# A hybrid decoder layer on one NeuronCore: another order of seven products, later background work at block seams, and other join and queue choices

## The chip, the cores and the metric

The kernel runs on one core of a Trainium2 chip. The metric is device time in microseconds: the median of three runs, 2982.76 us before the change (2982.41 to 2986.3).

## The reference

One layer of a decoder trunk is computed for a prompt of 2048 + 16 tokens and for 8 sample sequences of 8 tokens, with D = 1024 channels and F = 2816 hidden channels, all in float32:

```python
h = rmsnorm(x, norm1_g)
z = h @ w_in                                   # D -> 5D: za, zg, zp, gate_a, gate_b
a = za * sigmoid(zg)
a = layernorm(causal_dwconv(a, width 31) + conv_b)
a = silu(a) @ w_conv_out
p = trailing means of zp over 2/4/8/16 positions, minus zp; per-group linear map, scale
m = sigmoid(gate_a) * a + sigmoid(gate_b) * p
x = x + m @ w_out
h2 = rmsnorm(x, norm2_g)
up = causal_dwconv(h2 @ w_up, width 3)         # D -> 2F: value and gate
x = x + (gelu(gate) * value) @ w_down
y = rmsnorm(x, final_g)
```

The last rows of the convolution inputs, of the pooling inputs and of the up-projected rows are returned too.

## The kernel before

**Tiling.** Channels lie on the 128 partitions, in `KC` = 8 chunks; tokens lie along the free dimension. The tokens are cut into three blocks `b` = 0, 1, 2 of about 704 to 708 columns; the last holds the samples. A matmul has 128x128 weights and about 352 columns, half a block, so that one output chunk of a projection (a *unit*) is 8 chunks x 2 halves x 3 matmuls = 48 matmuls. Three, because each float32 product is made from a rounded high part and a low rest: low weight x high data, high x low, high x high (`gemm`). High and low parts are made by ACT (copy to fp32r) and DVE (subtract); weights are split once and written to DRAM (`keep`), and later blocks load both parts, 1 MB for a unit.

**Order of the units.** For each block: the projections for the convolution gate and value (`G_first`, `G`), the pooling inputs and gates (`PG`, with units `zp`, `wp`, gates), the convolution's output (`C`), the output projection (`WO`), the feed-forward part (`FF`, with up-projections `up` or `pair`, and down-projections `DN`). A block ends with its last `DN`, and the next block's `PG` follows: this is a block *seam*. For block 0 and block 2, `WO` and parts of the rest run in two halves of the columns, `FIRST` and `SECOND`. `join(first)` puts the units made since `first` into one group: their matmuls are then issued in turns, one chunk of each, instead of one unit after the other.

**Pairs.** In block 2, from the fourth hidden chunk on, value and gate of one hidden chunk are made together (`pair`): the 2x2 blocks of weights and data give four products' worth of work with seven products P1 to P7 of 12 matmuls each (Strassen's scheme in Winograd's form). `mixed_weights` prepares the sums of weight blocks in the background (tiles `raw`, stores `keep<-s`), and stores them as `m1` to `m4`. The seven products accumulate in four PSUM regions: `x` and `a` are the two halves of tile `ps1`, `bb` and `d` those of `ps2`. `sums` reads them back: `u` is made from `d`, `ug` (gate) from `u` and `bb`, `uv` (value) from `x`, `u` and `a`. `g_conv` and `v_post` apply the width-3 convolution, `g_conv` GELU too, and `fg_post` multiplies and splits.

**What sets the order.** The program is laid out by a planner while it is built. `Pace` keeps an estimated time for each engine; the costs are in the helpers (`tt`, `stt`, `act`, `load`, `store`, `mm`). Matmuls are issued unit after unit, and between units (inside a group, between turns) `drip` issues steps of background tasks as long as the estimated DVE time is behind TensorE's. A task may have a unit from which on it may start (`mark[...]`). `force` issues the rest of a task that a unit needs. Each engine works through its own queue in order; so do the DMA queues of SP (`load`) and POOL (`store`).

**Weights.** `w_loads` requests the weights of coming units: those that lie in DRAM in split form up to two units past the oldest unit in work (`LEAD` = 4), into four buffers (`W_BUFS`, tile `wb`). Two `raw` buffers take unsplit weights, and are shared with `mixed_weights`.

**Background tasks that the change touches.** `final(b)` makes y of block b (tiles `s`, stores `out_y`); `x_again(b)` loads the residual x of a block for `WO`, in which `add_post` adds it; `mixed_weights` is described above. The rsqrt of each norm is made with small matmuls, `ones` (column sums) and `cst` (spreading the result), with DVE steps on tile `rs` between them.

Of the kernel before, what the change touches and what calls it, by code (L numbers as in the profile page):

```python
# [133 lines left out]
def trunk(ctx: ExitStack, tc: tile.TileContext, A, O):  # L134
# [72 lines left out]

    def store(dst, src):
        nc.gpsimd.dma_start(out=dst, in_=src)  # L209
        move = size(src) * P * 4 / 340.0  # L210
        pace.put("pool", 1000.0, [], [src], late=2000.0 + move)
        pace.free["dma"] += move
# [563 lines left out]

    def x_again(b):
        for c in range(KC):
            R["x1", b, c] = x_load(b, c)
        yield  # L780

# [105 lines left out]
    def mixed_weights():  # L887
# [5 lines left out]
        for f in range(PLAIN, FC):  # L893
            yield from room(MIX_ROOM)
            v, g = (pace.alloc("raw", RAW_BUFS, wpool.tile([P, 2 * h], F32, tag="raw", name=nm("raw"), bufs=RAW_BUFS)) for _ in range(2))
            load(v, A["w_up"][f])
            load(g, A["w_up"][FC + f])
            a11, a12, a21, a22 = v[:, :h], v[:, h:], g[:, :h], g[:, h:]
# [16 lines left out]
            yield from part(a12, "m3", 0, 2 * h)  # L915
            yield from part(a22, "m3", h, 2 * h)
            s3 = S(h)
# [8 lines left out]
            yield from part(a11, "m2", h, 2 * h)  # L926
            yield from part(a12, "m4", 0, h)

# [55 lines left out]
    def pair(b, f):  # L984
# [9 lines left out]
        def mmf(_):  # L994
# [39 lines left out]
            def sums():  # L1034
                u = pu[:, n:]
                yield from ready(4)
                yield at(d)
                for k in ("c1", "c5", "c7"):
                    done(box[k])
                tt(u, pq[:, :n], d, ALU.add)  # L1040
                ug = S(2 * n)
                tt(ug[:, n:], pq[:, n:], pu[:, :n], ALU.add)
                tt(ug[:, n:], ug[:, n:], u, ALU.add)
                yield from ready(5)
                yield at(x)
                uv = S(2 * n)
                act(uv[:, :n], x, AF.Copy)
                yield from ready(6)
                yield at(bb)
                tt(ug[:, :n], u, bb, ALU.add)  # L1050
                two = lambda t: t.rearrange("p (a c) -> p a c", a=2)
                yield from g_conv(b, f, BOTH, two(ug))
                del ug
                yield from ready(7)
                yield at(a)
                tt(uv[:, n:], u, a, ALU.add)
                box.clear()
                del u
                yield at(uv)
                yield from v_post(b, f, BOTH, two(uv))  # L1060
                del uv
                yield from fg_post(b, f, BOTH)
# [21 lines left out]
            prod(x, 2, 0, b21, False)  # L1084
            box["n"] = 5
            yield
            for t in older:
                done(t)
            if pres[1]:
                pres[1]()  # L1090
            prod(bb, 2, h, mx[4], False)
            w_start(w[3])
            box["n"] = 6
            yield
            prod(a, 3, 0, b22, False)
            w_start(w[3] + 1)
# [8 lines left out]
    def final(b, ts_):  # L1105
        c0, c1 = cols(b, ts_)
        r = yield from (rstd_ps if b == NBLK - 1 and ts_[-1] == 1 else rstd_of)(x_part(b, ts_, "x2n"), c1 - c0)
        for c in range(KC):
            x = R["x1", b, c][:, c0:c1]
            o = wide(x, r) if len(r.shape) == 3 else x  # L1110
            calm = lambda: b == NBLK - 1 or pace.free["dma"] < pace.free["pe"]
            yield "room", calm
            stt(o, o, col(O_FG + c), r, ALU.mult, ALU.mult)
            store(O["y"][c, :, COL0[b] + c0 : COL0[b] + c1], x)
            if ts_[-1] == 1:
                del R["x1", b, c]
            yield
# [69 lines left out]
    def G_first(own):  # L1187

        halves = [(("h1", 0, FIRST),), (("h1", 0, SECOND),)]
        ws = [w_gate(0), w_value(0), w_gate(1)]  # L1190
        for ts_, nd in zip(SPLIT, halves):
            i = len(units)
            gate(0, 0, ws[0], nd, ts_)
            value(0, 0, ws[1], nd, ts_)
            join(i)
            gate(0, 1, ws[2], nd, ts_)
        n0, n1 = halves[1], (("h1", 1),)
        value(0, 1, w_value(1), n0)
        for c in range(2, KC):
# [30 lines left out]
    def PG(b, nd, ga):  # L1230
# [21 lines left out]
        zs = [c for g in POOL_ORDER for c in (2 * g, 2 * g + 1)]  # L1252
        for k in range(3):
            zp(zs[k])
        if b:
            join(i)
        zp(zs[3])
        for k, g in enumerate(POOL_ORDER):
# [27 lines left out]
    def WO(b, parts):  # L1286
        mark["WO", b] = len(units)
        for ts_ in parts:
            for c in range(KC):
                std_unit(  # L1290
                    W(("out", c), A["w_out"][c]), lambda: R["m", b], b, ts_,
                    lambda ps, c=c, ts_=ts_: add_post(b, c, ts_, ps, "x1n"), (("x", b),), wait=c == 0,
                    drop=("m", b) if ts_ == parts[-1] and c == KC - 1 else None,
                )

    def up(b, m, w, nd, ts_=BOTH, hold=None):
# [85 lines left out]
    for b in range(NBLK):  # L1382
# [5 lines left out]
        add_task(("s", b), silu(b), mark["mid", b] if b else mark["C", 0] - 2, [("cv", b)])  # L1388
        add_task(("x", b), x_again(b), mark["WO", b])
        for ts_ in parts.get(b, (BOTH,)):  # L1390
# [3 lines left out]
        for ts_ in SPLIT if b == NBLK - 1 else (BOTH,):  # L1394
            add_task(("y", b, ts_), final(b, ts_))
        if b + 1 < NBLK:
# [7 lines left out]
    add_task(("hist",), histories(), mark["WO", NBLK - 1])  # L1404
    add_task(("mw",), mixed_weights(), mark["PG", 1])

# [214 lines left out]
```

## Time and profile before

| | |
|---|---|
| median of three runs | 2982.76 us |
| the profiled execution | 2985.01 us |
| its span | 2983.2 us |
| TensorE (PE) busy | 2918.1 us, 98% |
| VectorE (DVE) busy | 2034.3 us, 68% |
| ScalarE (ACT) busy | 817.5 us, 27% |
| GpSimd (POOL) busy | 380.2 us, 13% |
| mean granted TensorE clock | 0.990 |
| DMA | 660.13 MB, mean 221 GB/s |

The profile lists each engine's instructions with start, duration, code line and the tiles written and read (`out<-in`, buffer numbers left out), and for an idle stretch what ended it. Most operations are recorded under the line of their helper: L215 is `mm`, L181 `tt`, L185 `stt`, L196 `act`, L205 `load`, L209 `store`. A busy TensorE is not one at full clock: the clock that was granted is given as a share, in stretches. A wait for several things is put down to the one that came last by the profile; where the engine named had long been done, it was another, often a DMA.

### The profile page before, as it was taken

To read this page: it belongs to the slowest core of one execution; us is meant where nothing else is said; L and a number is where in the kernel's file an instruction comes from. 1 tells how busy PE (TensorE), PEld (TensorE's weight loads), DVE (VectorE), ACT (ScalarE), POOL (GpSimd) and SP (SyncE) were. 2 spreads that over 40 slices of the span, in tenths; PEclk is the share of its full clock that TensorE was granted. 3 is DMA by queue.
4 is the path that set the end of the run, shared out by engine and by line. 5 is a ranking of instruction groups with operands and counts; after the bars stand their busy time and mean duration, and the time that the engine had idled before them with its cause. 6 is when DMAs were issued, how large, how long until landed. Compare 5 with 4: busy or idle time off the path is not lost.

```text
span 2983.2 us, 44492 instructions
## 1 busy us (share of the span) xinstructions
PE 2918.1 (98%) x17928; PEld 2906.2 (97%) x17928; DVE 2034.3 (68%) x3006; ACT 817.5 (27%) x1238; POOL 380.2 (13%) x730
## 2 busy tenths in 40 slices
PE   7999999999999999999999999999999999999997
PEld 7999999999999998999999999999999999999997
DVE  7998998679997456643499999646652136544645
ACT  4201334233223233522211213213241013221312
POOL 1111110020010102232110000222210010000001
PEclk9999999999999999999999999999999999999998
DMA  7424554965655657798643344879754384778786
GB/s 282 150 84 160 198 209 165 333 220 174 232 189 208 212 200 296 276 331 294 231 162 146 123 152 144 300 268 313 283 187 143 141 302 168 261 268 263 259 289 232
DMA packets 155501, 660.13 MB, mean 221 GB/s; under 512 B 24992, under 2 KB 29216, under 8 KB 113440
## 3 DMA queue, kind: packets, MB, share of 16 engines
q1 hardware_dynamic: 107280, 433.21, 43.0%
q0 software_dynamic: 48016, 224.09, 19.0%
q8 instruction: 141, 2.31, 0.3%
q14 instruction: 64, 0.52, 0.1%
HBM read 433.17 MB, written 224.05 MB: 220 GB/s over the span
## 4 chain that ended last, share of the span: by engine, by line
PE 85%; DVE 6%; issue 3%; DMA 3%; ACT 2%; POOL 1%; SPq 0%; DVEq 0%; POOLq 0%; ACTq 0%
PE ps L215 85%; DVE s L185 4%; DVE s L181 1%; DMA wb<-keep 1%; ACT s L196 1%; DVE wb L181 1%; POOL keep L209 1%; DMA raw<-in_w_in 1%; DMA raw<-in_w_up 0%; DMA s<-in_x 0%; DMA keep<-s 0%; ACT wb L196 0%; DMA raw<-in_w_out 0%; SPq L205 0%; DVE s L190 0%
## 5 line engine op out<-in xcount | busy, mean ns | idle before, releaser
L215 PE MATMUL ps<-s,wb 128*128 128x354 f32 (+3 forms) x17628 | 2885.0, 325 | 36.5 <-ACT s L196 14.5
L215 PEld LDWEIGHTS ps<-s,wb 128*128 128x128 f32 x17628 | 2867.4, 189 | 46.5 <-DVE s L181 18.2
L185 DVE SCALAR_TENSOR_TENSOR s<-s,half,s 128x704 f32<-128x704 f32 (+1 forms) x720 | 619.6, 925 | 0.0
L196 ACT ACTIVATE s<-s 128x704 fp32r<-128x704 f32 (+10 forms) x447 | 314.6, 711 | 808.2 <-DVE s L185 455.9
L181 DVE TENSOR_TENSOR s<-s,s 128x704 f32<-128x704 f32 (+11 forms) x526 | 400.7, 775 | 98.3 <-ACT s L196 89.9
L181 DVE TENSOR_TENSOR s<-s,ps 128x704 f32<-128x704 f32 (+4 forms) x225 | 158.8, 715 | 288.8 <-PE ps L215 246.8
L196 ACT ACTIVATE s<-ps 128x356 f32<-128x356 f32 (+5 forms) x197 | 117.0, 600 | 683.7 <-PE ps L215 650.7
L185 DVE SCALAR_TENSOR_TENSOR s<-ps,cst,s 128x704 f32<-128x704 f32 (+1 forms) x188 | 178.2, 949 | 110.9 <-ACT s L196 107.2
L209 POOL DMA_DIRECT2D keep<-s x266 | 142.3, 540 | 640.4 <-ACT s L196 507.8
L185 DVE SCALAR_TENSOR_TENSOR s<-s,cst,s 128x708 f32<-128x708 f32 (+4 forms) x188 | 156.0, 842 | 88.0 <-ACT s L196 82.0
L181 DVE TENSOR_TENSOR wb<-raw,wb 128x1024 fp32r<-128x1024 f32 (+3 forms) x136 | 153.0, 1126 | 41.8 <-ACT wb L196 41.2
L196 ACT ACTIVATE wb<-raw 128x1024 fp32r<-128x1024 f32 (+3 forms) x136 | 132.4, 978 | 165.2 <-PE ps L215 88.4
L196 ACT ACTIVATE s<-ps,cst 128x704 f32<-128x704 f32 (+1 forms) x94 | 79.1, 844 | 329.7 <-PE ps L215 322.9
L209 POOL DMA_DIRECT2D keep<-wb x136 | 77.1, 567 | 690.0 <-DVE wb L181 673.6
L185 DVE SCALAR_TENSOR_TENSOR s<-s,ps 128x704 f32<-128x704 f32 (+6 forms) x65 | 43.8, 694 | 147.8 <-PE ps L215 136.1
L185 DVE SCALAR_TENSOR_TENSOR s<-s,s 128x704 f32<-128x704 f32 (+2 forms) x96 | 85.2, 888 | 70.9 <-ACT s L196 68.2
L181 DVE TENSOR_TENSOR s<-raw,s 128x512 fp32r<-128x512 f32 x114 | 74.2, 686 | 33.6 <-ACT s L196 25.7
L196 ACT ACTIVATE s<-raw 128x512 fp32r<-128x512 f32 x114 | 67.6, 623 | 39.4 <-PE ps L215 18.6
L181 DVE TENSOR_TENSOR s<-s 128x718 f32<-128x718 f32 (+6 forms) x64 | 55.1, 861 | 25.8 <-issue 15.3
L209 POOL DMA_DIRECT2D out_ffn_s<-sf x44 | 23.7, 538 | 316.7 <-ACT sf L196 270.3
L185 DVE SCALAR_TENSOR_TENSOR sc<-sa,cst,sc 128x64 f32<-128x64 f32 x232 | 47.0, 279 | 0.3
L196 ACT ACTIVATE s<-s,half 128x704 f32<-128x704 f32 (+1 forms) x48 | 46.3, 971 | 0.8
(61 smaller groups left out, 465.9 us busy)
## 6 DMA issues: line engine op xcount, KB each, us to landing
wb<-keep SPq DMA_DIRECT2D x227, 1024.0 KB, 5.0
keep<-wb POOLq DMA_DIRECT2D x100, 1024.0 KB, 6.4
keep<-s POOLq DMA_DIRECT2D x266, 256.0 KB, 5.2
raw<-in_w_up SPq DMA_DIRECT2D x82, 512.0 KB, 6.4
wb<-keep SPq DMA_DIRECT2D x40, 640.0 KB, 5.1
wb<-keep SPq DMA_DIRECT2D x32, 768.0 KB, 5.4
raw<-in_w_in SPq DMA_DIRECT2D x40, 512.0 KB, 4.6
s<-in_x SPq DMA_DIRECT2D x40, 352.0 KB, 7.7
```

The source lines that it names most:

```text
L181: nc.vector.tensor_tensor(out=out, in0=a, in1=b, op=op)
L185: nc.vector.scalar_tensor_tensor(out=out, in0=a, scalar=s, in1=b, op0=op0, op1=op1)
L196: nc.scalar.activation(out, a, func, **kw)
L209: nc.gpsimd.dma_start(out=dst, in_=src)
L215: nc.tensor.matmul(out, lhsT=lhsT, rhs=rhs, start=start, stop=stop, skip_group_check=again)
```

## The change

Seven edits are made together.

1. In `pair`, P3 into `a` comes sixth and P4 into `bb` seventh (before: P4 sixth, P3 seventh). `m3` and `m4` swap one of their blocks for it, and `sums` does the value side before the gate side.
2. In `PG`, for blocks 1 and 2, two `zp` units are joined instead of three.
3. `final(b)` of blocks 0 and 1 may start only six units after the next block's `PG` begins, and `mixed_weights` six units after that of block 1.
4. `mixed_weights` loads its raw weights through POOL's queue (`load_later`) instead of SP's; in `Pace` a store counts 600 ns of POOL's time instead of 1000.
5. The residual x is loaded by the `WO` units: three chunks ahead of the first unit, then one chunk at each unit, two units early. It was a task that loaded all eight ahead of the first. In `WO` of blocks 0 and 2 the first two units of the first half are joined.
6. In `G_first`, `value(0, 1)` is made in halves, the first of them with the first half's units.
7. The stores of y of the last block go through SP's queue instead of POOL's.

```diff
+    def load_later(out, src):
+        nc.gpsimd.dma_start(out=out, in_=src)
+        move = size(out) * P * 4 / 340.0
+        pace.put("pool", 600.0, [out], [], late=2000.0 + move)
+        pace.free["dma"] += move
-    def store(dst, src):
-        nc.gpsimd.dma_start(out=dst, in_=src)
+    def store(dst, src, last=False):
+        (nc.sync if last else nc.gpsimd).dma_start(out=dst, in_=src)
-        pace.put("pool", 1000.0, [], [src], late=2000.0 + move)
+        pace.put("pool", 600.0, [], [src], late=2000.0 + move)
...
-    def x_again(b):
-        for c in range(KC):
-            R["x1", b, c] = x_load(b, c)
-        yield
+    def x_again(b, c):
+        for k in range(0 if c == 0 else c + 2, min(c + 3, KC)):
+            R["x1", b, k] = x_load(b, k)
...
-            load(v, A["w_up"][f])
-            load(g, A["w_up"][FC + f])
+            load_later(v, A["w_up"][f])
+            load_later(g, A["w_up"][FC + f])
...
-            yield from part(a22, "m3", h, 2 * h)
+            yield from part(a22, "m4", 0, h)
...
-            yield from part(a12, "m4", 0, h)
+            yield from part(a12, "m3", h, 2 * h)
...
-                yield from ready(5)
-                yield at(x)
+                yield from ready(6)
+                yield at(a)
                 uv = S(2 * n)
                 act(uv[:, :n], x, AF.Copy)
-                yield from ready(6)
+                tt(uv[:, n:], u, a, ALU.add)
+                yield at(uv)
+                two = lambda t: t.rearrange("p (a c) -> p a c", a=2)
+                yield from v_post(b, f, BOTH, two(uv))
+                del uv
+                yield from ready(7)
                 yield at(bb)
                 tt(ug[:, :n], u, bb, ALU.add)
...
                 yield from g_conv(b, f, BOTH, two(ug))
                 del ug
-                yield from ready(7)
-                yield at(a)
-                tt(uv[:, n:], u, a, ALU.add)
...
-                yield from v_post(b, f, BOTH, two(uv))
...
-            prod(bb, 2, h, mx[4], False)
+            prod(a, 2, h, b22, False)
             w_start(w[3])
             box["n"] = 6
             yield
-            prod(a, 3, 0, b22, False)
+            prod(bb, 3, 0, mx[4], False)
...
-            store(O["y"][c, :, COL0[b] + c0 : COL0[b] + c1], x)
+            store(O["y"][c, :, COL0[b] + c0 : COL0[b] + c1], x, b == NBLK - 1)
...
-        ws = [w_gate(0), w_value(0), w_gate(1)]
+        ws = [w_gate(0), w_value(0), w_gate(1), w_value(1)]
...
             gate(0, 1, ws[2], nd, ts_)
+            value(0, 1, ws[3], nd, ts_)
...
-        value(0, 1, w_value(1), n0)
...
-        for k in range(3):
+        for k in range(4):
             zp(zs[k])
-        if b:
-            join(i)
-        zp(zs[3])
+            if b and k == 1:
+                join(i)
...
-                    lambda ps, c=c, ts_=ts_: add_post(b, c, ts_, ps, "x1n"), (("x", b),), wait=c == 0,
+                    lambda ps, c=c, ts_=ts_: add_post(b, c, ts_, ps, "x1n"), (), wait=c == 0,
+                    pre=(lambda c=c: x_again(b, c)) if ts_ == parts[0] else None,
...
+                if c == 1 and ts_ == FIRST:
+                    join(mark["WO", b])
...
-        add_task(("x", b), x_again(b), mark["WO", b])
...
-            add_task(("y", b, ts_), final(b, ts_))
+            add_task(("y", b, ts_), final(b, ts_), mark["PG", b + 1] + 6 if b + 1 < NBLK else 0)
...
-    add_task(("mw",), mixed_weights(), mark["PG", 1])
+    add_task(("mw",), mixed_weights(), mark["PG", 1] + 6)
```

More of the change, by code (lines that the diff above doesn't have):

```diff
@@ L1043, in sums @@
                 tt(ug[:, n:], ug[:, n:], u, ALU.add)
-                yield from ready(5)
-                yield at(x)
+                yield from ready(6)
+                yield at(a)
                 uv = S(2 * n)
                 act(uv[:, :n], x, AF.Copy)
-                yield from ready(6)
+                tt(uv[:, n:], u, a, ALU.add)
[4 more added lines that the diff above has]
+                yield from ready(7)
                 yield at(bb)
                 tt(ug[:, :n], u, bb, ALU.add)
-                two = lambda t: t.rearrange("p (a c) -> p a c", a=2)
+                box.clear()
+                del u
                 yield from g_conv(b, f, BOTH, two(ug))
                 del ug
-                yield from ready(7)
-                yield at(a)
-                tt(uv[:, n:], u, a, ALU.add)
-                box.clear()
-                del u
-                yield at(uv)
-                yield from v_post(b, f, BOTH, two(uv))
-                del uv
                 yield from fg_post(b, f, BOTH)
@@ L1084, in mmf @@
             prod(x, 2, 0, b21, False)
-            box["n"] = 5
             yield
```

## The prediction, made before the changed kernel ran

> **What bounds the kernel now.** I read the page first, then TensorE's waits and timeline, then single stretches. TensorE is busy 98% of the span, so only its idle gaps and slow-clock stretches can be won; no matmul is removed.
>
> ```profile
> span 2983.2 us, 44492 instructions
> PE 2918.1 (98%) x17928; PEld 2906.2 (97%) x17928; DVE 2034.3 (68%) x3006; ACT 817.5 (27%) x1238; POOL 380.2 (13%) x730
> ```
>
> All idle time is 2983.2 - 2918.1 = 65.1 us. TensorE's timeline (start, duration, line, operation, count, idle before and what ended it) says where the parts that this edit can reach lie:
>
> ```profile
> 31.57 0.80 PE L215 MATMUL ps<-ones,s 128*128 128x1 f32 x6 [0.87 <-DVE s L181]
> 34.41 1.55 PE L215 MATMUL ps<-cst,rs 128*128 128x128 f32 x6 [2.04 <-DVE rs L185]
> 37.68 0.67 PE L215 MATMUL ps<-s,wb 128*128 128x358 f32 x1 [1.72 <-ACT s L196]
> 553.79 0.66 PE L215 MATMUL ps<-s,wb 128*128 128x352 f32 x1 [2.42 <-ACT s L196]
> 554.72 34.31 PE L215 MATMUL ps<-s,wb 128*128 128x352 f32 x194 [0.26 <-DVE s L181]
> 1173.06 280.79 PE L215 MATMUL ps<-s,wb 128*128 128x352 f32 x1728 [7.24 <-ACT s L196]
> 2153.88 278.52 PE L215 MATMUL ps<-s,wb 128*128 128x354 f32 x1704 [4.92 <-DMA wb<-keep]
> 2465.55 3.90 PE L215 MATMUL ps<-s,wb 128*128 128x356 f32 x12 [2.87 <-DMA wb<-keep]
> 2645.28 13.92 PE L215 MATMUL ps<-s,wb 128*128 128x356 f32 x84 [0.60 <-DVE s L181]
> ```
>
> A gap can cost more than its length. Rows of stretches (bounds, length, busy and count of each engine, granted clock, DMA share, GB/s):
>
> ```profile
> 553.40:560.20 6.80, 6.15 (x20) 5.77 (x21) 2.55 (x3) 2.42 (x4) 0.53 (x1) 0.50 1.02 375
> 560.20:575.00 14.80, 14.80 (x92) 14.80 (x92) 5.94 (x9) 5.09 (x7) 1.60 (x3) 1.00 0.87 324
> 1173.00:1178.00 5.00, 4.94 (x17) 4.97 (x18) 4.08 (x5) 1.90 (x3) 1.83 (x4) 0.50 0.99 338
> 2154.20:2157.60 3.40, 3.40 (x14) 3.40 (x13) 2.44 (x6) 0.90 (x2) 0.78 (x1) 0.50 0.96 370
> 2640.00:2700.00 60.00, 57.60 (x350) 56.41 (x350) 39.22 (x70) 22.43 (x52) 4.84 (x9) 1.00 0.74 263
> ```
>
> At full clock one matmul takes 14.80/92 = 0.161 us. After the three larger gaps the clock is 0.50: 6.15 - 20 x 0.161 = 2.9 us lost at 553, 4.94 - 17 x 0.161 = 2.2 at 1173, 3.40 - 14 x 0.161 = 1.1 at 2154. The 0.60 us gaps of the pairs leave it at 1.00.
>
> The Trainium skill, "TensorE: Matmul & The Clock Gate", Part 1 (the HAM clock gate), has the half clock come after at least one idle window of about 3.4 us. The trace disagrees at 553, where 2.42 us were enough. By the rule the 2.9 us there would not hang on the gap, and the sum below would be 2.9 us smaller, ending at 2954.0. I give it no chance of its own, because the row shows the loss.
>
> **The change part by part.**
>
> *Product order in a pair.* A product is 12 matmuls, 12 x 0.166 = 2.0 us (13.92/84 each). In before the order ends P2, P4, P3; P4 writes `bb`, which shares a PSUM tile with `d`, and DVE still has to read `d` for `u`:
>
> ```profile
> 2643.89 0.90 DVE L181 TENSOR_TENSOR s<-s,s 128x708 f32<-128x708 f32 x1
> 2644.70 0.52 DVE L181 TENSOR_TENSOR s<-s,ps 128x356 f32<-128x356 f32 x1
> 2645.52 0.45 ACT L196 ACTIVATE s<-ps 128x356 f32<-128x356 f32 x1
> 2647.55 0.52 DVE L181 TENSOR_TENSOR s<-s,ps 128x356 f32<-128x356 f32 x1 [0.52 <-PE ps L215]
> 2653.85 0.79 ACT L196 ACTIVATE s<-s 128x708 f32<-128x708 f32 x1
> 2654.53 0.88 ACT L196 ACTIVATE s<-s,cst 128x708 f32<-128x708 f32 x1
> 2655.44 1.95 DVE L185 SCALAR_TENSOR_TENSOR s<-s,cst,s 128x708 f32<-128x708 f32 x2 [3.04 <-ACT s L196]
> 2657.48 0.25 DVE L190 TENSOR_SCALAR s<-sf,cst 128x64 f32<-128x64 f32 x1
> 2657.77 0.60 DVE L185 SCALAR_TENSOR_TENSOR s<-sf,cst,s 128x64 f32<-128x64 f32 x2
> PE ps L215 <- DVE s L181: 9.1, 15, 0.7
> ```
>
> `u` ends at 2644.70 + 0.52 = 2645.22, TensorE goes on at 2645.28, and 2.0 us later DVE adds `bb` (2647.55). The read is late because the previous pair's `fg_post` (2643.89) stands before it in DVE's queue. The last line, TensorE's waits from 2500 to 2921, counts 15 such gaps, 9.1 us. Afterwards P3 stands between: it writes the other tile, whose `x` and `a` were copied long ago, and gives 2.0 us of cover for a gap of 0.60. The older pair's chain moves too: value side from P3's end, gate side from P4's. Counting P4's end as 0: `uv` from -1.9 (0.52), ACT's scaling 0.88, two STT 1.95 and the samples 0.25 + 0.60 bring the value side to 2.3; then `ug` 0.52, ACT 0.88, STT 1.95, samples 0.85, GELU 0.79 and the product 0.90 end at 8.2. The next pair's `d` is ready at 8.0 (four products), so `u` runs from 8.2 to 8.7, and P4, which waits for it, starts only at 12: 3 us of slack. Who waits for the added P3: only the gate side, which DVE could not start before 2.3 anyway. Gain 9.1 us. Ends: 9.1 at best; at worst P3, in the tile that also holds `x`, waits for ACT's copy of `x` (0.45) in each of 19 pairs, which takes 8.6. I take 9.1, as that copy is issued behind P3. After the last pair the longer chain (GELU now last) stands ahead of the last down-projection's fifth row: +0.4, between 0 and 0.8 (GELU's row).
>
> *Seams (`PG` joins two, not three; `final` and `mixed_weights` start 6 units later; raw loads on POOL's queue).*
>
> ```profile
> 1134.61 25.48 SPq L205 DMA_DIRECT2D raw<-in_w_up  x4
> 1163.95 31.25 SPq L205 DMA_DIRECT2D wb<-keep  x7
> wb<-keep SPq DMA_DIRECT2D x1, 1024.0 KB, 9.0
> 2119.33 23.87 SPq L205 DMA_DIRECT2D raw<-in_w_up  x4
> 2143.29 10.45 DMA wb<-keep
> wb<-keep SPq DMA_DIRECT2D x227, 1024.0 KB, 5.0
> ```
>
> ACT is named for the 7.24 us, but that ACT work was long past for a fourth `zp`. Its weights were: issued at 1163.95 (the third row is that load alone), landed 9.0 us later, 1172.95; TensorE started at 1173.06. At the second seam SP stood 23.87 us in four raw loads waiting for buffers; the weight load behind them left at 2143.29 and took 10.45, 2153.74, against 2153.88. A median load takes 5.0. The load window reaches two units past the oldest, so three joined units leave the fourth's load until the group is through. With two joined, the third's weights are there already and cover the fourth's load: 48 x 0.161 = 7.7 us from the group's end, with no raw load ahead on SP and no y burst beside it. 7.7 beats 5.0; at 9.0 some 1.3 us would be left. Gain 7.24 + 2.2 = 9.4 and 4.92 + 1.1 = 6.0. Ends: 0 to 15.4; I take all, since the row of 5.0 is the one without the burst.
>
> What is pushed on: `final`'s 8 STT and 8 stores and the start of the mixed weights move by six units, five of 48 matmuls and one of 24, 264 x 0.161 = 42.5 us, into projections where a DMA share of 0.95 left TensorE busy throughout (first row below). On POOL a raw load stands behind stores that wait for the same DVE subtraction; it adds its issue, 38 times about 0.53 us (4.25/8, the row of the last stores), to a queue that is 13% busy. Behind it wait weight stores and the history copies of `pool_post` (a rival below). The last raw loads are the four at 2119; 42.5 us later is covered by the stretch of the second row, ahead of the pairs:
>
> ```profile
> 1275.00:1350.00 75.00, 75.00 (x468) 75.00 (x467) 32.65 (x47) 21.51 (x34) 23.64 (x45) 1.00 0.95 339
> 2250.00:2325.00 75.00, 75.00 (x465) 75.00 (x464) 10.75 (x12) 8.67 (x11) 0.00 (x0) 1.00 0.39 141
> ```
>
> So nothing; were that cover gone, up to 42.5 us would be forced ahead of the first pair.
>
> *`WO`: first two units joined, x in chunks.* Block 0's first unit has 7 x 3 = 21 matmuls before it needs the last merged chunk, whose `hi` and `lo` end the 2.42 and 0.26 gaps. Joined, another 21 x 0.161 = 3.4 us stand there. 2.68 < 3.4: gain 2.68 + 2.9 = 5.6, ends 2.4 (clock stays slow) and 5.6; I take 5.6. Block 2 shows no gap there. The second unit's post comes one unit later; PSUM has two more slots. Chunks: three x loads ahead, then one per unit two units early, 2 x 24 x 0.161 = 7.7 us, against
>
> ```profile
> 541.08 7.89 SPq L205 DMA_DIRECT2D s<-in_x  x8
> s<-in_x SPq DMA_DIRECT2D x40, 352.0 KB, 7.7
> ```
>
> in a burst of eight. Nothing; without that cover about 1 us. SP's queue gains: a raw output weight no longer waits behind eight x loads (7.89).
>
> *Start.* 24 matmuls (24 x 0.166 = 4.0 us) of `value(0, 1)` now need only the first half and can stand in the gaps of 0.87, 2.04 and 1.72. Put ahead of the `ones` matmuls they fill the first alone; between `ones` and `cst`, the second. Ends 0.9 and 4.0; I take 1.0, the planner's likelier place being ahead.
>
> *Last stores on SP.*
>
> ```profile
> 2974.54 4.25 POOL L209 DMA_DIRECT2D out_y<-s  x8 [10.87 <-DVE s L185]
> out_y<-s POOLq DMA_DIRECT2D x8, 177.0 KB, 2.5
> s<-in_x SPq DMA_DIRECT2D x16, 179.0 KB, 4.1
> ```
>
> POOL's last issue ends at 2978.8 (2974.54 + 4.25), the span at 2983.2, though a store lands in 2.5. On SP the first half's stores wait for DVE; the last down-projection weights are requested ahead of them, so nothing stands behind. No row shows an SP store. From 2.3 us less (it lands as POOL's and the end follows) to 1.6 more (4.1 in place of 2.5); I take 1.0 less. The planner's costs (1000 to 600) only reorder what is issued; I take nothing, and 2 us either way, as the small gaps of the quoted timeline (0.26 to 2.04) are of that size.
>
> **Not touched:** the gap of 2.87 us at 2465 waits for a third up-projection's weights; neither window nor order changes there.
>
> **Sum.** 9.1 - 0.4 + 9.4 + 6.0 + 5.6 + 1.0 + 1.0 = 31.7 us. The profiled execution took 2985.01 us (span 2983.2), so 2953.3 for it; it stands 2.25 above the median of 2982.76, so the median becomes 2982.76 - 31.7 = 2951.1.
>
> **The rivals.**
>
> *Contention stays.* The Trainium skill, "DMA: Bandwidth & Descriptors", Rules for kernel authors, says that spreading DMAs over issuing engines saves issue time only, since all run on the same 16 DMA engines. As a mechanism here: the loads of 9.0 and 10.45 us stay so long because stores still fill the engines (0.99 of their time at 1173 to 1178), and both seam gaps remain or return six units on. Then 31.7 - 15.4 = 16.3, giving 2966.5. For it: the 9.0; against: one unit more of lead, and the stretch at 0.95 without a gap. 14%.
>
> *The pairs' wait only moves.* Tile-wide waits could catch P3 behind the copy of `x`, which is ACT work of 0.45. Then 9.1 is not won: 2960.2. Against: the copy is issued only after P3. 9%.
>
> *POOL's queue blocks (the other side).* Behind a raw load that waits for its buffer stand the small history copies that a `zp`'s post needs. SP's waits of 1100 to 1200:
>
> ```profile
> SPq L205 <- DVE s L181: 18.3, 3, 9.0
> ```
>
> If all of a 9.0 us wait reached TensorE for each of 19 f, 171 us: 2982.8 - 31.7 + 171 = 3122. It decides from 31.7/19 = 1.7 us per f. With one unit (7.8 us) ready meanwhile, 1.2 us x 19 = 23 remains and the kernel is still faster, 2974. Slower 5%.
>
> *No gain:* fresh gaps from the reshuffled plan use up everything, 2983. 4%.
>
> **How the numbers follow.** Forecast 68%; the rivals as above. From no change this kernel is told within about 0.2% (6 us). Contention to 2966.5 and unmoved pairs set the upper end, 2967; below, the full 4.0 at the start and 2.3 at the end (4.3 more), and 2 of the planner give 2945. Faster: 68 + 14 + 9 = 91, less 1 for rivals together: 0.90; same 0.04; slower 0.06.
>
> **What would show it.** Pairs: TensorE's waits from the first pair to the last without the 15 gaps of 0.60. Seams: no gap over 1 us between the first `zp` units and the fifth, clock 1.00 there. `WO`: no gap and no 0.50 at the first output projection. End: SP, not POOL, in the last lines of the chain. Unchanged: the gap before the first joined up-projections of block 2. Wrong, if gaps named "DMA wb<-keep" stand elsewhere, or POOL copies appear in the chain.

## The result, and the profile after

The changed kernel takes 2966.74 us (median; 2964.97 to 2968.08) against 2982.72 for the kernel before in the same series: ratio 0.9943, 95% interval 0.9926 to 0.9961. It is 16.0 us faster; 31.7 were forecast. The profiled execution took 2964.97 us. Its page, the lines for span and engines:

```profile
span 2963.1 us, 44420 instructions
PE 2913.6 (98%) x17928; PEld 2906.4 (98%) x17928; DVE 2034.2 (69%) x3007; ACT 818.3 (28%) x1238; POOL 393.9 (13%) x752
```

TensorE's timeline after the change, where idle time is left or was to go (start, duration, line, operation, count, idle before and what ended it; `issue` means that the profile shows nothing it waited for):

```profile
544.84 37.19 PE L222 MATMUL ps<-s,wb 128*128 128x352 f32 x230
627.50 0.66 PE L222 MATMUL ps<-s,wb 128*128 128x354 f32 x1 [1.81 <-ACT s L196]
892.12 2.68 PE L222 MATMUL ps<-s,ones 128*128 128x352 f32 x4 [4.72 <-DVE s L181]
1636.44 5.83 PE L222 MATMUL ps<-s,wb 128*128 128x354 f32 x25 [3.76 <-issue]
2599.72 60.48 PE L222 MATMUL ps<-s,wb 128*128 128x354 f32 x371
2912.16 0.43 PE L222 MATMUL ps<-s,wb 128*128 128x354 f32 x1 [2.32 <-ACT s L196]
```

The same places as rows of stretches (bounds, length, busy and count of PE, PEld, DVE, ACT, POOL, granted clock, DMA share, GB/s):

```profile
627.50:634.30 6.80, 6.19 (x20) 5.82 (x21) 6.80 (x15) 3.34 (x7) 6.63 (x8) 0.50 0.00 0
890.30:897.10 6.80, 4.97 (x13) 4.01 (x14) 5.04 (x6) 1.85 (x3) 1.07 (x2) 0.50 0.94 321
1150.00:1175.00 25.00, 25.00 (x158) 25.00 (x157) 9.71 (x11) 4.43 (x6) 3.11 (x6) 1.00 0.32 106
1637.80:1641.20 3.40, 3.40 (x14) 3.40 (x13) 1.69 (x3) 2.03 (x3) 0.00 (x0) 0.50 0.00 0
2125.00:2160.00 35.00, 35.00 (x218) 35.00 (x217) 25.32 (x41) 10.80 (x24) 16.66 (x34) 1.00 0.90 313
```

The gap of 553 is gone (544.84 runs 37.19 us unbroken), both seams run full at clock 1.00 (25.00 of 25.00, 35.00 of 35.00, the latter with the DMA engines at 0.90), and 60 us of the pairs have no gap (371 matmuls in 60.48 us). Three stalls are new: at 627, at 892 and at 1636, each with the clock at 0.50 behind it.

To see what each was worth, count all 17928 matmuls in order of time and compare the start of the same number in both traces:

| matmul | before, us | after, us | shift, us | what lies between this row and the one above |
|---|---|---|---|---|
| 200 | 58.49 | 57.10 | -1.4 | start: 1.4 won |
| 3300 | 562.77 | 556.10 | -6.7 | 553: 5.3 won |
| 3700 | 627.66 | 621.51 | -6.2 | |
| 3800 | 646.07 | 643.54 | -2.5 | new stall at 627: 3.6 lost |
| 5400 | 906.14 | 910.96 | +4.8 | new stall at 892: 7.3 lost |
| 7000 | 1163.12 | 1168.83 | +5.7 | |
| 7300 | 1221.10 | 1215.90 | -5.2 | seam 1: 10.9 won |
| 8900 | 1477.63 | 1472.00 | -5.6 | |
| 10000 | 1654.45 | 1654.95 | +0.5 | new stall at 1636: 6.1 lost |
| 13000 | 2137.80 | 2140.51 | +2.7 | |
| 13300 | 2193.07 | 2187.90 | -5.2 | seam 2: 7.9 won |
| 15000 | 2476.24 | 2468.98 | -7.3 | |
| 17600 | 2910.03 | 2891.59 | -18.4 | pairs: 11.2 won |
| end of the span | 2983.2 | 2963.1 | -20.1 | end: 1.7 won |

Won: 1.4 + 5.3 + 10.9 + 7.9 + 11.2 + 1.7 = 38.4. Lost in the three new stalls: 3.6 + 7.3 + 6.1 = 17.0. The unlabelled rows add 1.1 of loss, together 20.3, which rounding takes to 20.1. Every gain of the forecast shows at its place; something took back 17 us. (Such shifts between two single executions carry about 2 us of chance: two kernels below whose TensorE order is the same differ by 2.1 us at matmul 4000. The two spans differ by 20.1 us, the medians by 16.0: the traced execution of before lay 2.3 us above its median, that of the change 1.8 below.)

### The profile page after: what moved, and what is told of

It reads as the page before. It is cut to its first block, busy times and chain, and to the rows that moved or that the text cites. A ratio compares the mean times of both kernels' runs of the same rounds, so it can differ in the third digit from the quotient of the medians.

```text
span 2963.1 us, 44420 instructions
## 1 busy us (share of the span) xinstructions
PE 2913.6 (98%) x17928; PEld 2906.4 (98%) x17928; DVE 2034.2 (69%) x3007; ACT 818.3 (28%) x1238; POOL 393.9 (13%) x752
## 4 chain that ended last, share of the span: by engine, by line
PE 71%; DVE 12%; issue 10%; DMA 3%; POOL 2%; ACT 1%; SPq 0%; DVEq 0%; POOLq 0%; ACTq 0%
PE ps L222 71%; DVE s L185 7%; DVE s L181 3%; DVE wb L181 2%; POOL keep L216 2%; DMA wb<-keep 1%; DMA raw<-in_w_up 1%; DMA keep<-s 1%; ACT s L196 1%; DMA keep<-wb 0%; ACT wb L196 0%; POOL raw L210 0%; DMA s<-in_x 0%; SPq L205 0%; DVE rs L185 0%
## 5 line engine op out<-in xcount | busy, mean ns | idle before, releaser
L181 DVE TENSOR_TENSOR s<-s,s 128x704 fp32r<-128x704 f32 (+11 forms) x526 | 401.1, 775 | 126.2 <-ACT s L196 117.3
L196 ACT ACTIVATE s<-ps 128x356 f32<-128x356 f32 (+6 forms) x197 | 117.3, 601 | 694.3 <-PE ps L222 677.6
```

What stands on the lines that cost most here:

```text
L181: nc.vector.tensor_tensor(out=out, in0=a, in1=b, op=op)
L196: nc.scalar.activation(out, a, func, **kw)
```

## The experiments

Each series ran on one chip together with the kernel before: 2982.22 (first four), 2982.46 (next four), 2981.34 (last four). "Edit" numbers are those of the section on the change; a line of three dots in a code cut stands for lines left out.

**1. Edit 1 alone.** The kernel before with the new order of products:

```diff
 # pair: P3 into a sixth, P4 into bb seventh; sums: value side, then gate side
+            prod(a, 2, h, b22, False)
...
+            prod(bb, 3, 0, mx[4], False)
...
```

> Before, with the new order of the seven products alone. Theory (the pairs' wait sits behind DVE's read of d in P4's tile): all 15 gaps of 0.60 us between the first and the last pair go, TensorE's count through that stretch gets 9 to 10.4 us shorter, nothing else moves, 2982.7 - 9 = 2972 to 2974. Rival (it only moves): gaps of similar size before P2 or P3, 2980 to 2984.

2971.41 us, ratio 0.9970 (0.9958 to 0.9982): 10.8 us, 0.6 below the range of the theory. All 15 gaps of 0.60 are gone. Both seam gaps stay, and at the first one the profile now names the weights, where in the trace before it had named ACT:

```profile
1171.49 8.76 PE L215 MATMUL ps<-s,wb 128*128 128x352 f32 x37 [8.39 <-DMA wb<-keep]
2152.76 7.55 PE L215 MATMUL ps<-s,wb 128*128 128x354 f32 x34 [5.15 <-DMA wb<-keep]
```

The prediction's reading, that the release by ACT was long past and a weight load was the cause, is borne out.

**2. Edit 2 alone.** Two `zp` units joined, not three, in the kernel before:

```diff
-        for k in range(3):
+        for k in range(4):
             zp(zs[k])
-        if b:
-            join(i)
-        zp(zs[3])
+            if b and k == 1:
+                join(i)
```

> Before, with two zp units joined instead of three and nothing else. Theory A (the fourth zp's weights are late at both seams, and what TensorE wins ahead of 1600 us it loses again near 1636, where its PSUM waits for a backlog on DVE): the 7.24 us gap near 1166 shrinks to 1 to 5 us since raw loads still stand on SP, the 4.92 us gap near 2149 stays at 3 to 5 us, and a new gap near 1636 takes most of the first gain: 2979 to 2983. Rival B (gains add up, the gap near 1636 belongs to another edit): no gap near 1636, 2972 to 2978.

2966.40 us, ratio 0.9951 (0.9937 to 0.9966): 15.8 us, from the smallest of the edits, and 5.6 us below the range of B, the nearer theory. SP's queue and TensorE at the first seam, TensorE at the second:

```profile
1155.41 17.02 SPq L205 DMA_DIRECT2D wb<-keep  x4
1164.21 15.97 PE L215 MATMUL ps<-s,wb 128*128 128x352 f32 x98 [0.17 <-DMA wb<-keep]
2134.72 25.45 PE L215 MATMUL ps<-s,wb 128*128 128x354 f32 x156
```

The weight loads begin at 1155, not at 1163.95, and 0.17 us is left of 7.24; the second seam runs through. (In before, 25 us of raw loads stand ahead of the load of 1163.95 in SP's queue. They do not hold it: in experiment 3, without them, it leaves at 1164.20.) `final` and `mixed_weights` still start where they did, so neither had to move for this. There is no stall at 1636 either, as rival B had it: that one belongs to another edit.

**3. Raw loads of edit 4 alone.**

```diff
...
-            load(v, A["w_up"][f])
-            load(g, A["w_up"][FC + f])
+            load_later(v, A["w_up"][f])
+            load_later(g, A["w_up"][FC + f])
```

> Before, with the raw loads of mixed_weights on POOL's queue and nothing else. Theory A: the gap near 2149 goes (6 us with the slow clock), since SP no longer stands in raw loads; the gap near 1166 stays at 5 to 7 us, because there the buffer of the first joined unit and a 9 us landing set it: 2976 to 2978. Rival (the contention of the y burst sets both): both gaps stay, 2982 to 2984.

2990.51 us, ratio 1.0031 (1.0020 to 1.0043): 8 us slower, above both ranges. SP and TensorE at the first seam, then POOL, DVE and TensorE at the second:

```profile
1164.20 20.65 SPq L205 DMA_DIRECT2D wb<-keep  x5
1175.13 5.17 PE L222 MATMUL ps<-s,wb 128*128 128x352 f32 x22 [9.06 <-DMA wb<-keep]
...
2138.97 1.09 POOL L210 DMA_DIRECT2D raw<-in_w_up  x2
2156.15 0.54 POOL L216 DMA_DIRECT2D keep<-s  x1 [0.54 <-DMA out_y<-s]
2156.68 0.21 POOL L201 COPY s<-phist 128x15 f32<-128x15 f32 x1
2156.93 1.73 DVE L181 TENSOR_TENSOR s<-s 128x658 f32<-128x658 f32 x2 [4.99 <-POOL s L201]
2166.45 0.66 PE L222 MATMUL ps<-s,wb 128*128 128x354 f32 x1 [3.13 <-ACT s L196]
```

The first seam keeps its gap, now 9.06 us; at the second the old gap is gone and others come. A history copy of 0.21 us stands behind stores of y and `keep` stores that themselves wait for work on DVE and for other transfers; it runs at 2156.68, DVE waits 4.99 us for it, and TensorE for what DVE and ACT make of it. Before, the same copy ran at 2144.13. This is the prediction's rival "POOL's queue blocks", at one place and not in each of 19 pairs. It is not all of the 8 us: against the trace before, 6.7 us are won at the old gap and 8.3 lost at the new ones there, 1.0 is lost at the first seam and 1.9 at 2097, where TensorE waits 1.76 us for weights. Together that is 4.5; the rest was not found.

**4. The change without edit 5** (x loaded by a task ahead of `WO`, no join in `WO`; the rest as changed):

```diff
...
+        add_task(("x", b), x_again(b), mark["WO", b])
...
-                if c == 1 and ts_ == FIRST:
-                    join(mark["WO", b])
```

> The changed kernel without edit 5 (x loaded as one task, first two output units not joined). Theory A: the 5.3 us won near 553 are lost, the slow clock near 627 (3.6 us) and the 4.72 us gap near 892 (7.9 us with its clock) do not come up, so TensorE reaches 1600 us some 6 us earlier than in the changed kernel, but DVE has as much to do by then, the gap near 1636 grows from 3.76 to about 10 us and the total stays at 2965 to 2968. Rival B (losses add up locally): the gap near 1636 stays at about 3.8 us and the total is 2959 to 2962.

2952.34 us, ratio 0.9902 (0.9887 to 0.9917), against 0.9926 to 0.9961 for the whole change: 14.4 us faster than it, and 6.7 below the lower range, since both theories kept the stall at 1636. TensorE's timeline without edit 5:

```profile
552.22 0.42 PE L222 MATMUL ps<-s,wb 128*128 128x352 f32 x1 [2.55 <-ACT s L196]
553.14 33.04 PE L222 MATMUL ps<-s,wb 128*128 128x352 f32 x194 [0.50 <-DVE s L181]
627.85 1.70 PE L222 MATMUL ps<-s,wb 128*128 128x354 f32 x9
629.85 0.43 PE L222 MATMUL ps<-s,wb 128*128 128x354 f32 x1 [0.30 <-ACT s L196]
631.12 268.60 PE L222 MATMUL ps<-s,wb 128*128 128x354 f32 x1655 [0.83 <-DVE s L181]
```

The gap at 553 is back; the 1.81 us at 627 are 0.30, since nine matmuls (1.70 us) stand there between the norm's `cst` matmuls and the first unit that needs the norm; and 1655 matmuls run from 631 to 900 without the stall at 892. Nor is there one at 1636. So all three new stalls come with edit 5, which in the table wins 5 us and loses 17.

**5. The stall at 892 moved away** in the whole change:

```diff
 # conv_norm, before rsums(acc, W)
-        yield at(acc)
+        yield "at", pace.ready(acc) + (6000.0 if b == 1 else 0.0)
```

> The changed kernel, with one addition: for block 1 the step of conv_norm that issues the column sums (ones) counts as ready 6 us later for the planner, which puts these four matmuls 78 matmuls further back in TensorE's order, where they stood before the change. Theory A (the stall at 892 us is the price of that place in the order, and of nothing else): the gap of 4.72 us and the half clock behind it go, about 7 us, and the stalls at 627 and 1636 stay: 2958 to 2962. Theory B (DVE is late in this stretch whatever the place; the wait returns at the cst matmuls or at the following posts): gaps of 4 to 8 us in all between 890 and 960, 2964 to 2968.

2965.35 us, ratio 0.9940 (0.9924 to 0.9957): no different from the change. Why the place matters: DVE's last two additions in the change, then the same in before, with TensorE's four column sums there:

```profile
890.16 1.81 DVE L181 TENSOR_TENSOR s<-s,s 128x704 f32<-128x704 f32 x2
897.53 1.81 DVE L181 TENSOR_TENSOR s<-s,s 128x704 f32<-128x704 f32 x2
902.34 1.35 PE L215 MATMUL ps<-s,ones 128*128 128x352 f32 x4
```

The additions end at 890.16 + 1.81 = 891.97 and at 899.34. In before the column sums came 3 us later, 902.34. In the change they stand 78 matmuls (78 x 0.161 = 12.6 us) earlier in TensorE's order, and their row, 892.12 with 4.72 idle, is the wait for the additions. With the 78 matmuls given back the gap of 4.72 is gone, and matmul 5500 starts 7.9 us earlier than in the change (1.6 of it from before that place). But the order behind 945 us is the same, and yet new stalls stand at 1969 and 2097, which take it back: at matmul 13000 the kernel is 2.7 us later than the change. For the first of them, ACT, DVE and TensorE:

```profile
1961.35 1.16 ACT L196 ACTIVATE s<-raw 128x512 fp32r<-128x512 f32 x2 [7.56 <-DMA raw<-in_w_up]
1963.89 0.83 ACT L196 ACTIVATE s<-ps,cst 128x704 f32<-128x704 f32 x1
1967.41 1.93 DVE L185 SCALAR_TENSOR_TENSOR s<-ps,cst,s 128x704 f32<-128x704 f32 x2
1969.44 10.82 PE L222 MATMUL ps<-s,wb 128*128 128x352 f32 x56 [3.74 <-issue]
```

ACT waits 7.56 us for a raw weight. A read of PSUM stands behind it in ACT's queue, and DVE, which needs what ACT makes of the weight, has reads of PSUM behind that in its own; these end at 1967.41 + 1.93 = 1969.34, and TensorE goes on at 1969.44. Theory A is right about the cause of the stall at 892. The median lies in B's range, but not for B's reason: between 890 and 960 the largest gap is 0.81 us. How often the new stalls come is not shown: the traced execution took 2969.73 us, 4.4 above the median, and another 2959.59, inside A's range.

**6. Edit 5 alone**, both parts, in the kernel before:

```diff
...
-        add_task(("x", b), x_again(b), mark["WO", b])
...
+                    pre=(lambda c=c: x_again(b, c)) if ts_ == parts[0] else None,
+                if c == 1 and ts_ == FIRST:
+                    join(mark["WO", b])
```

> The kernel before with edit 5 alone: x loaded chunk by chunk and the first two units of WO joined in blocks 0 and 2. Theory A (the edit costs the same alone as in company, 14.4 us net: 5 won at 553, lost at 627, at 892, and at 1636): 2993 to 2999, with the ones matmuls of block 1 waiting near 910 and a new gap between the first seam and the second of block 1's output projection. Theory B (only some of its stalls are its own; the one at 1636 needs the delayed final as well): 2986 to 2991. Theory C (it is a gain alone, its losses come from company): 2976 to 2981.

2987.57 us, ratio 1.0020 (1.0010 to 1.0029): by itself the edit makes the kernel slower by 5 us. The number is B's, but not for B's reason: all three stalls are there, at 629 (1.81), 893 (5.25) and 1646 (3.78), and it loses less than A said because the gap at the second seam, 4.92 us before, is 0.50 here:

```profile
1646.20 203.69 PE L215 MATMUL ps<-s,wb 128*128 128x354 f32 x1248 [3.78 <-issue]
2168.55 267.82 PE L215 MATMUL ps<-s,wb 128*128 128x354 f32 x1649 [0.50 <-DVE s L181]
```

**7. The change without the x chunks** (eight loads ahead of `WO`, as before; the join stays):

```diff
...
+        add_task(("x", b), x_again(b), mark["WO", b])
...
-                    pre=(lambda c=c: x_again(b, c)) if ts_ == parts[0] else None,
```

> The changed kernel with x loaded as before, eight chunks ahead of WO, but the first two WO units of blocks 0 and 2 still joined. The ones matmuls of block 1's convolution norm stay at their early place; block 1's second norm returns to its place of before. Theory A (the stall at 1636 comes from the chunks, which alone move block 1's order; the rest is the join's): gap at 1636 gone, about 5 us; no gap at 553, gap at 892 there: 2960 to 2964. Theory B (the chunks only save SP's queue from a burst of eight loads and have no cost): the burst returns as a wait for weights near the output projections: 2966 to 2971.

2958.77 us, ratio 0.9926 (0.9911 to 0.9941): theory A, whose range it misses by 1.2 us. The stall at 1636 is gone; that at 892 is there (4.80 us). DVE in the stretch of the third stall, first the change, then without chunks; the last line is TensorE without chunks:

```profile
1594.60 1.02 DVE L185 SCALAR_TENSOR_TENSOR s<-s,ps 128x354 f32<-128x354 f32 x3 [7.05 <-PE ps L222]
1619.20 15.28 DVE L185 SCALAR_TENSOR_TENSOR s<-s,half,s 128x644 f32<-128x644 f32 x19
1634.41 3.77 DVE L185 SCALAR_TENSOR_TENSOR s<-ps,cst,s 128x704 f32<-128x704 f32 x4
...
1611.27 14.48 DVE L185 SCALAR_TENSOR_TENSOR s<-s,half,s 128x644 f32<-128x644 f32 x18
1625.68 3.77 DVE L185 SCALAR_TENSOR_TENSOR s<-ps,cst,s 128x704 f32<-128x704 f32 x4
1574.80 65.38 PE L222 MATMUL ps<-s,wb 128*128 128x354 f32 x402
```

In the change DVE stands 7.05 us idle before an operation that was put too early in its queue. The time is missing afterwards: 19 convolution steps of the background stand ahead of the four PSUM reads at 1634.41, and TensorE goes on at 1636.44. Without the chunks DVE does not wait, reads at 1625.68, and TensorE runs through.

**8. The change without edit 5, raw loads on SP again** (the cost of 600 for a store stays):

```diff
...
-            load_later(v, A["w_up"][f])
-            load_later(g, A["w_up"][FC + f])
+            load(v, A["w_up"][f])
+            load(g, A["w_up"][FC + f])
...
```

> The changed kernel without edit 5 (both parts) and with mixed_weights loading its raw weights on SP's queue again, as before; the cost of 600 for a store stays. The same without this, raw loads on POOL, took 2952.34. Theory A (raw loads on POOL cost 8 us alone, because history copies wait behind them; that cost is still paid in company): 2943 to 2947. Theory B (with two units joined neither queue is late, so the place of the raw loads is worth nothing): 2950 to 2955. Theory C (on SP they again hold up weight loads at the seams although two units are joined): gaps named DMA wb<-keep near 1170 and 2150, 2956 to 2964.

2947.06 us, ratio 0.9885 (0.9871 to 0.9900), the shortest of all, 19.7 us under the change. No gap is named at the seams. Against experiment 4 it is 5.3 us less; the two intervals overlap, and the time falls between A and B, close to A. Not all of the 5.3 can be the queue's. Of the 7.4 us between the two traces, 2.6 arise at 553, ahead of the first raw load on POOL (1170.7), and 1.5 at 2443, behind the last (2157.6); behind both gaps the clock halves in experiment 4 and not here. That leaves some 3 us.

**9. The whole change with raw loads on SP**, edit 5 kept:

```diff
...
-            load_later(v, A["w_up"][f])
...
+            load(v, A["w_up"][f])
...
```

> The changed kernel with mixed_weights loading its raw weights on SP's queue, as before; all else of the change stays. TensorE's order is the same in both. Theory A (a raw load on POOL's queue takes 8.3 us to land, and ACT, whose queue is in order, waits 123 us for these loads where it waited 12 before; behind it stand reads of PSUM): ACT's waits for raw fall below 40 us, and the time to 2959 to 2963, with the stalls at 627, 892 and 1636 unmoved. Theory B (the 5 us between the two kernels without edit 5 were mostly another run of the same thing; ACT has the slack): 2965 to 2968.

2963.01 us, ratio 0.9939 (0.9927 to 0.9952): not to be told from the change. ACT's waits for raw weights in before, in the change, and here (us in total, times, longest):

```profile
ACT s L196 <- DMA raw<-in_w_up: 12.1, 10, 2.6
ACT s L196 <- DMA raw<-in_w_up: 122.9, 21, 23.6
ACT s L196 <- DMA raw<-in_w_up: 64.2, 16, 21.4
```

The time lies on A's edge, but its reason did not hold: the waits only halve, and the shift against the change, -2.1 us at matmul 4000, stays between -1.8 and -2.7 up to 13000, while the first raw load on POOL comes only after 7000. Nor does such a load land later: between 1180 and 2150 us the median is 8.6 us on POOL in the change and 8.9 on SP before. What is left is when it is requested, which was not followed load by load, and the order: by operation and tile, 233 of DVE's 3010 places differ between the two kernels. ACT can afford most of the wait; where PSUM reads stand behind it (experiment 5) it cannot.

**10. Edit 5's join, with the order behind it held** (in the kernel of experiment 8):

```diff
+                if c == 1 and ts_ == FIRST:
+                    join(mark["WO", b])
-        yield at(acc)
+        yield "at", pace.ready(acc) + (6000.0 if b == 1 else 0.0)
```

> The kernel without edit 5 and with raw loads on SP (2947.06), and in it the first two WO units of blocks 0 and 2 joined; block 1's column sums count as ready 6 us later for the planner, so that from there on (about 925 us) every queue has the same order as without the join, and only the stretch from 553 to 925 us differs. Theory A (edit 5 costs by the places it gives in the order, and by nothing else): the gaps of 1.4 and 0.5 us at 552 go, some 2 to 4 us are lost near 627, and from 925 on nothing: 2946 to 2950. Theory B (a shift of a few us in time, with the same order, is enough for new stalls): new gaps after 925 us, 2952 to 2957.

2951.68 us, ratio 0.9903 (0.9888 to 0.9918), 1.7 us above A's range and 0.3 below B's, but with A's picture: no gap at 553 and 1.81 us at 628; against experiment 8 the shift is -0.3 us at matmul 3500, +2.8 at 4000, between 2.6 and 3.9 until 2440 us, and 4.4 at matmul 15000, behind a gap where the clock halves here and not in experiment 8. With the same order behind it, a few us of delay cost little but themselves over 1500 us. (That is no rule: in the trace of experiment 5 a shift alone sufficed for new stalls, with raw loads on POOL.) The join saves little here, since the gaps it closes are 1.44 and 0.50 us in experiment 8.

**11. Edit 3 undone** in the kernel of experiment 8:

```diff
-            add_task(("y", b, ts_), final(b, ts_), mark["PG", b + 1] + 6 if b + 1 < NBLK else 0)
-    add_task(("mw",), mixed_weights(), mark["PG", 1] + 6)
+            add_task(("y", b, ts_), final(b, ts_))
+    add_task(("mw",), mixed_weights(), mark["PG", 1])
```

> The kernel without edit 5 and with raw loads on SP (2947.06), and in it final(0), final(1) and mixed_weights start where they did before, not six units later: edit 3 undone. Theory A (two joined units instead of three are all that empties the two seam gaps; the six units are worth nothing): 2945 to 2949, no gap over 1 us near 1170 and 2150. Theory B (the stores of y and the raw loads crowd the seams, and two joined units win only because these are out of the way): gaps named DMA wb<-keep at one or both seams, 2951 to 2960.

2952.27 us, ratio 0.9905 (0.9891 to 0.9918), 5.2 us above experiment 8, with overlapping intervals. That is in B's range, and at the first seam B's gap comes back: 1.43 us of waiting for weights, 1.9 us of shift from matmul 6000 to 7300. At the second seam there is none:

```profile
1163.47 278.00 PE L215 MATMUL ps<-s,wb 128*128 128x352 f32 x1728 [1.43 <-DMA wb<-keep]
```

But of the 5.8 us between the two traces, 3.2 arise at 553, where edit 3 has not begun, and at 2443: there the clock halves here and not in experiment 8, behind gaps of nearly the same length (last section). So the six units are worth a little at the first seam; how much in all stays open.

**12. Edits 6 and 7 alone** (second value in halves at the start, last stores on SP):

```diff
...
+            value(0, 1, ws[3], nd, ts_)
...
-        value(0, 1, w_value(1), n0)
...
-            store(O["y"][c, :, COL0[b] + c0 : COL0[b] + c1], x)
+            store(O["y"][c, :, COL0[b] + c0 : COL0[b] + c1], x, b == NBLK - 1)
```

> The kernel before with edits 6 and 7 alone: value(0, 1) made in halves at the start, the last stores of y on SP. Theory A (the two terms as the lag between the traces has them, 1.4 at the start and 1.9 at the end): 2978.8 to 2979.8. The forecast's own terms (1.0 and 1.0): 2980.5. Theory B (the start's 24 matmuls only change places, and the end follows the longest store on either queue): 2982 to 2983.

2977.80 us, ratio 0.9987 (0.9978 to 0.9995): 3.5 us against the kernel before of its series, at A's 3.3 and above the 2.0 of the forecast. In the change SP's 16 stores of y end at 2959.9, and the span 3.2 us later; in before POOL's ended at 2978.8, and the span 4.4 us later.

## Why the prediction was half right

*The number: luck in part.* 2951.1 us was forecast and 2966.74 measured, 0.3 us inside the upper end of the range, 2967. That end was set by two rivals, contention and unmoved pairs, that did not come true. What kept the time up, some 17 us of new stalls, had no term in the sum.

*Pairs: right.* Forecast 9.1 less 0.4; alone 10.8. P3 gives the cover, nothing waits for the added steps, and a copy of `x` does not catch P3. About 2 us more were won than the gaps are long. They may lie in the matmuls behind a gap: one takes 60.48/371 = 0.1630 us in the change and took 57.60/350 = 0.1646 in the stretch of before, which over the 19 x 84 = 1596 matmuls of the pairs makes 2.5 us. That was not tried by itself. The longer chain at the end showed, but 1.2 us long where the sum had 0.4, between 0 and 0.8: 2.32 us at 2912 where 1.10 stood before.

*Seams: right, and by the join alone.* Forecast 15.4; measured 15.8 alone. The rival "contention stays" gave 2966.5 and the kernel came out at 2966.74, but that is a coincidence: its mechanism, both gaps remaining, is contradicted by the rows of 1150 and 2125, where TensorE is busy in 25.00 of 25.00 and 35.00 of 35.00 us, the second at a DMA share of 0.90. The Trainium skill, "DMA: Bandwidth & Descriptors", Rules for kernel authors (issuing from more engines saves issue time alone), agrees with experiment 3: with the raw loads on another queue the weights of the first seam still took 10.80 us to land, the DMA engines being busy for 1.00 of the time (1165 to 1175), and left a gap of 9.06 us.

*Start and end: right in sign.* 2.0 forecast, 3.5 measured.

*Sum of these.* Alone they bring 10.8 + 15.8 + 3.5 = 30.1; together (experiment 11, which holds edits 1, 2, 6, 7 and the new cost of a store) 2981.34 - 2952.27 = 29.1. The parts add up, as the sum supposed.

*`WO`: this step failed.* The term read "gain 5.6", and 5.3 did arrive at 553, though about half of it by chance: experiment 1, with nothing changed there, passes the same gap 2.3 us cheaper than before, since its clock stays at 1.00. The price was put at nothing: "the second unit's post comes one unit later; PSUM has two more slots", and for all reordering "2 us either way". It was 17.0 us in the three stalls of the table (by the medians the edit costs 14 net of its gain), none of them at the edited units: the first two 70 and 340 us behind block 0's join, the third some 200 us behind block 1's x loads (1402 to 1461 in the change). The planner lays out one order for five engines from its own clock; an edit that moves this clock by a unit can place later background steps anew, and here did. Three of these places were bad: the second norm's `cst` matmuls with nothing behind them to cover ACT's copy of the result (627), column sums 12.6 us earlier than before (892), a post too early in DVE's queue (1636). The mechanism was on the list, as the rival "fresh gaps from the reshuffled plan" at 4%, sized at the whole gain; it was the case, sized at half of it. Without the chunks, 8 of the 14 us that the edit costs in company are gone (2958.77); the chunks without the join were not tried.

*Raw loads on POOL: the rival was a real one.* "Adds its issue", costed at nothing, is 8 us slower alone. In company it is between nothing (experiment 9) and 5.3 us (8 against 4), of which some 3 can be its own. The new cost of a store was not tried by itself.

*Six units later:* costed at nothing; worth 5.2 us at most, of which 1.9 show at the first seam; not settled.

*Signs named beforehand.* "Wrong, if gaps named DMA wb<-keep stand elsewhere, or POOL copies appear in the chain": neither came as something new: a gap of 1.59 us at 2904 is named so, but it stood in before (1.71 at 2924), and so did the gap at 2459 (2.54, 2.87 in before) that the prediction left alone; the landing of raw weights, not POOL's copies, stands in the chain of waits with 1% of the span. The stalls that did come are named DVE, ACT and "issue", for which the prediction had set no sign.

## What to carry to other kernels

Where a program writes out one order for several in-order queues, cost an edit twice: at its place, and by the order that it leaves behind it. Compare the two orders before arguing about the time: a small matmul that moves by 78 places towards its operands, or a read that gets behind fifteen microseconds of background work, can be seen without a chip. And try the edits one at a time: here the parts add up to within 1 us, one of them costs 14, and leaving it and the raw loads on POOL out (2947.06) more than doubles the gain.

## What was not expected of the hardware

The half clock does not follow from a gap's length. Gap and clock behind it: at 553 in experiments 8, 11 and 1, then at one later place in experiment 8 and in before (timeline rows and stretches):

```profile
551.25 0.42 PE L215 MATMUL ps<-s,wb 128*128 128x352 f32 x1 [1.44 <-ACT s L196]
552.17 31.50 PE L215 MATMUL ps<-s,wb 128*128 128x352 f32 x194 [0.50 <-DVE s L181]
552.20:555.60 3.40, 3.40 (x21) 3.40 (x22) 1.63 (x2) 0.50 (x1) 0.53 (x1) 1.00 1.01 393
550.82 0.43 PE L215 MATMUL ps<-s,wb 128*128 128x352 f32 x1 [1.49 <-ACT s L196]
551.75 33.06 PE L215 MATMUL ps<-s,wb 128*128 128x352 f32 x194 [0.50 <-DVE s L181]
553.00:556.50 3.50, 3.50 (x14) 3.50 (x14) 0.41 (x1) 0.50 (x1) 0.53 (x1) 0.51 0.99 381
553.40:556.80 3.40, 2.88 (x16) 2.64 (x17) 2.55 (x3) 1.42 (x2) 0.53 (x1) 1.00 1.01 418
2443.24 2.16 PE L215 MATMUL ps<-s,wb 128*128 128x356 f32 x12 [2.90 <-DMA wb<-keep]
2443.24:2446.64 3.40, 3.40 (x23) 3.40 (x24) 0.54 (x4) 0.00 (x0) 0.00 (x0) 1.00 0.53 217
2464.83:2475.07 10.24, 9.52 (x35) 9.55 (x36) 1.65 (x10) 0.30 (x1) 0.00 (x0) 0.50 0.25 100
```

Gaps of 1.44 and 0.50 us left the clock at 1.00 (experiment 8), gaps of 1.49 and 0.50 halved it for 3.4 us (11), and gaps of 2.48 and 0.50 left it at 1.00 (1). At the later place a gap of 2.90 left it at 1.00 in experiment 8, and one of 2.87 in before was followed by 10.2 us at 0.50. The Trainium skill, "TensorE: Matmul & The Clock Gate", Part 1, has the clock watched in a free-running window of about 3.4 us, whose phase differs from run to run; that fits the spread, and the length of the slow stretches, but not its demand of a whole idle window. For a forecast this means that what a slow clock costs behind a gap of 1.5 to 3 us cannot be read from one trace: the 553 gap of before cost 5.6 us by its row (2.68 idle and 2.9 of slow clock), and that of experiment 8 cost 1.9, all of it idle.
